# A transformer block on one Trainium2 core: part of the first shift and scale sums moved to TensorE, and the second half of them queued behind the first products

## The chip, the cores and the metric

The kernel runs on one core of a Trainium2 chip. The metric is device microseconds of one execution, the median of several runs. The core's engines appear under the names of the profile: PE is TensorE (PEld its weight loads), DVE is VectorE, ACT is ScalarE, POOL is GpSimd, SP is the engine that issues most DMAs.

## The reference

One layer of a block with 512 tokens of width 1024. A conditioning vector `c` gives shift, scale and gate vectors, the input is normalised and modulated by them, and one wide projection follows, which feeds two attention branches; a retrieval layer with 16384 single-neuron experts ends the block. Only the start matters here:

```
mod = silu(c) @ w_ada + b_ada                 # w_ada is 1024 x 6144
sh1, sc1, g1, sh2, sc2, g2 = split(mod, 6)
h = rms_norm(x, norm1_g) * (1 + sc1) + sh1    # 512 x 1024
proj = h @ w_in                               # 1024 contraction = 8 tiles of 128
```

So no element of `h` exists before its shift and scale are known, and each of these is a sum over 1024 rows of `w_ada`.

## The kernel before, in words

Loads. SP first asks for `x` (4 transfers) and then for the 2048 columns of `w_ada` that hold sh1 and sc1 (L166 to L174). These come in four chunks of 512 columns, in the order shift of the first half, scale of the first half, shift of the second half, scale of the second half (`i` = 0, 2, 1, 3). A chunk is four tiles `wa` of 512 KB; a tile holds two of the eight pieces `k` of the contraction. There are eight buffers for the sixteen `wa` tiles, so the tiles of the third and fourth chunk are asked for as those of the first two come free.

Sums. For a chunk (L284 to L299) POOL makes piece 0 times its `silu(c)` value (`accw`), DVE adds further pieces, one SCALAR_TENSOR_TENSOR of 128x512 each (L292), and TensorE sums over the 128 partitions: four matmuls of one column with `accw` as weights and a column of ones (L297). The pieces named in `PK` don't go through DVE: TensorE multiplies them directly, four matmuls of one column each, on the same line. In fp32 the trace shows eight instructions for four of these. A DVE reduce (L299) adds the parts up, and `ada_fin` (L216) adds the bias and, for a scale, forms (1 + scale) times the gain. Before, `PK = (1,)`: one piece in eight for every chunk.

Modulation. TensorE transposes the normalised `x` into eight contraction tiles `kt` (L267, four transposes each, two PSUM buffers), ACT copies each out to `xT` (L286). Once a shift and its scale are there, `mod_split` (L270) makes four of the tiles: DVE multiplies and adds (L274), ACT rounds the result to the high part `hh` (L91), DVE subtracts to get the low part `hl` (L92). Tiles 0 to 3 follow the first two chunks, tiles 4 to 7 the last two.

Products. `proj` (L378) takes the pieces of `w_in`, splits each into `whi` and `wlo` in the same way (L91, L92; low parts on POOL or DVE, `piece`, L370) and multiplies: for each of the eight contraction tiles, four row blocks by three matmuls of 512 columns (`mm3`, L84 to L88), so 12 products a tile and 96 in all for the first 512 columns (`v_chunk(1536, 512, ...)`, called at L674). All four PSUM tiles `pj` hold its sums until the eighth tile is done; then ACT copies them to `va` (L479) and the next chunk can begin.

Order. The program is written with the tile framework. Within an engine the instructions run in one fixed order, which the framework chooses when the program is built, from the order in the text and its own estimate of times; nothing is reordered on the chip but for weight loads pulled ahead. In the text the first projection comes far behind the sums, behind the rotary tables too.

Of the kernel before, what the change touches and what calls it, by code (L numbers as in the profile page):

```python
# [15 lines left out]
F32 = mybir.dt.float32  # L16
F32R = mybir.dt.float32r
# [43 lines left out]
def setup(tc, ctx, K):  # L61
# [22 lines left out]
    def mm3(ps, l, r, start, stop):  # L84
        (lh, ll), (rh, rl) = l, r
        nc.tensor.matmul(ps, lh, rh, start=start, stop=False)  # L86
        nc.tensor.matmul(ps, lh, rl, start=False, stop=False)  # L87
        nc.tensor.matmul(ps, ll, rh, start=False, stop=stop)  # L88

    def split(hi, lo, raw, eng=None):  # L90
        nc.scalar.activation(hi, raw, AF.Copy)  # L91
        (eng or nc.vector).tensor_tensor(lo, raw, hi.bitcast(F32), op=OP.subtract)  # L92

    def rsqrt(out, v, w):
        i = K.wk.tile([128, w], I32, name=f"rs_i{w}", bufs=2)
# [36 lines left out]
def front(K, A):  # L132
# [15 lines left out]
    def wraw():  # L148
        return wf.tile([128, 512], F32, name="raw", bufs=5)
# [120 lines left out]
    def mod_split(raws, col, dst, hook=None, kts=range(8)):  # L270
        for kt in kts:
            raw = raws(kt)
            t = f2()
            nc.vector.tensor_scalar(t, raw, col[:, 8 + kt:9 + kt], col[:, kt:kt + 1], op0=OP.mult, op1=OP.add)  # L274
            split(dst[0][:, kt, :], dst[1][:, kt, :], t)
            if hook is not None:
                hook(kt, t)

    norm_rows(xt, xt, "n1", st)
    PK = (1,)  # L280
    xT = st.tile([128, 8, 512], F32, name="xT")
    hT = K.big("h", ta)
    col1 = cst.tile([128, 16], F32, name="col1")
    for n, i in enumerate((0, 2, 1, 3)):  # L284
        for kt in range(2 * n, 2 * n + 4) if n % 2 == 0 else ():
            nc.scalar.activation(xT[:, kt, :], transpose_in(xt, kt, ptr()), AF.Copy)  # L286
        accw = st.tile([128, 512], F32, name="acc0", bufs=2)
        w = [wa[4 * n + k // 2][:, k % 2, :] for k in range(8)]
        nc.gpsimd.tensor_scalar(accw, w[0], sil[:, 0:1], 0.0, op0=OP.mult, op1=OP.add)
        for k in range(1, 8):  # L290
            if k not in PK:
                nc.vector.scalar_tensor_tensor(accw, w[k], sil[:, k:k + 1], accw, op0=OP.mult, op1=OP.add)  # L292
        p = pscore()
        sums = [(w[k], sil[:, k:k + 1]) for k in PK] + [(accw, ones[:, 0:1])]
# [71 lines left out]
    win = A['w_in'].rearrange("(k p) n -> p k n", p=128)  # L366
    nload = [0]
    ND1 = 20

    def piece(load, n, pool=None):  # L370
        raw = wraw()
        hi, lo = ((pool or wf).tile([128, 512], F32R, name=s, bufs=2 if pool else 4) for s in ("whi", "wlo"))
        load(raw)
        nload[0] += 1
        split(hi[:, :n], lo[:, :n], raw[:, :n], nc.gpsimd if nload[0] % 2 and not 8 <= nload[0] < ND1 else nc.vector)
        return hi[:, :n], lo[:, :n]

    def proj(lT, wv, c0, n, nk, done, jp=None):  # L378
        pss = [pmat()[:, :n] for _ in range(4)]
        for k in range(nk):  # L380
            if jp is None:
                w = piece(lambda raw: nc.sync.dma_start(raw[:, :n], wv[:, k, c0:c0 + n]), n)
            else:
                w = piece(lambda raw: nc.sync.dma_start(
                    raw[:, :n].rearrange("p (g i) -> p g i", g=3),
                    wv[:, k, c0:c0 + 768].rearrange("p (g j i) -> p g j i", g=3, j=2)[:, :, jp, :]), n)
            for a in range(4):
                at = slice(a * 128, a * 128 + 128)
                l = [t[k] if type(t) is list else t[:, k] for t in lT]
                mm3(pss[a], (l[0][:, at], l[1][:, at]), w, k == 0, k == nk - 1)  # L390
            yield 12 * 0.216 * n / 512
        for a in range(4):
            done(a, pss[a])

    att = Pool("att")
    oa = att.tile([128, 4, 256], F32, name="oa")
# [114 lines left out]
    for i in range(2):  # L511
# [4 lines left out]
            nc.gpsimd.memset(b[z, :], 0.0)  # L516
            q.append(b)
        qraw.append(q)
    va = dil.tile([128, 4, 768], F32, name="va")

    def k_raw(p):
        raw = dil.tile([128, 512], F32, name="kT", bufs=4)
# [33 lines left out]
    def dil_out(j, a, s, rz):  # L556
# [8 lines left out]
        for b in range(6):  # L565
            hd = (j, j, j, j, 4 + j, 8 + j)[b]
            kt = b if b < 4 else a
            nc.tensor.matmul(po[:, :64], eT[:, b * 128:b * 128 + 128], va[:, kt, hd * 64:hd * 64 + 64],
                             start=b == 0, stop=b == 5)
        nc.vector.tensor_scalar(oa[:, a, j * 64:j * 64 + 64], po[:, :64], rz, None, op0=OP.mult)  # L570

# [705 lines left out]
```

## Time and profile before

| | us |
|---|---|
| median of 3 runs | 2010.34 (2009.19 to 2011.33) |
| the profiled execution, its own time | 2011.68 |
| its span in the profile | 2009.8 |
| PE busy in the span | 1873.7 (93%) |
| DVE busy | 1593.2 (79%) |
| ACT busy | 842.7 (42%) |
| POOL busy | 698.0 (35%) |

The profile is of one execution. Its page gives the busy time of each engine, the span in 40 slices of 50.2 us with the busy share in tenths, and the granted TensorE clock in the same slices. A view of stretches gives the same for any part of the span; a view in order of time lists instructions with their start, their length (of a merged run of like instructions: from the first start to the last end), their line, and in brackets the time that the engine sat idle before them and what ended it.

### The profile page before, as it was taken

What the parts mean: (1) busy time and instruction counts of PE and PEld (TensorE: products, weight loads), DVE (VectorE), ACT (ScalarE), POOL (GpSimd) and SP (SyncE); (2) the same over time, 40 slices, a digit from 0 to 9 for tenths busy, and PEclk for the clock granted to TensorE, in tenths of its full rate; (3) what the DMA queues carried; (4) which work ended last, traced back from release to release, by engine and by line L of the source; (5) the groups of instructions that cost most, each with busy time, mean ns of one, the idle gap of its engine ahead of it and who ended that gap; (6) DMA issues with size and microseconds to landing.
All of it is one profiled execution on the core that took longest, in us unless ns stands there. A gap on an engine that the chain in (4) does not pass through costs nothing.

```text
span 2009.8 us, 28332 instructions
## 1 busy us (share of the span) xinstructions
PE 1873.7 (93%) x9858; PEld 1620.1 (81%) x9858; DVE 1593.2 (79%) x3276; ACT 842.7 (42%) x1330; POOL 698.0 (35%) x534
## 2 busy tenths in 40 slices
PE   6999998989899899999989999839999999999998
PEld 5987777778677788899989999828888888878886
DVE  7488585886775759999979989968778888888764
ACT  3444454645633333345545555513333333333342
POOL 2554332352235522012444147233234334323200
PEclk9999999999999999999999999969999999999999
DMA  7334242122256322468688979889999999999962
GB/s 262 86 120 121 63 145 60 35 87 84 59 152 215 128 72 81 147 226 276 229 295 316 322 274 322 299 287 371 360 320 354 342 354 330 355 361 325 345 225 93
DMA packets 206417, 447.30 MB, mean 223 GB/s; under 512 B 17297, under 2 KB 104642, under 8 KB 206146
## 3 DMA queue, kind: packets, MB, share of 16 engines
q1 hardware_dynamic: 168592, 309.14, 45.5%
q0 software_dynamic: 36864, 134.23, 18.8%
q10 hardware_dynamic: 818, 2.12, 0.3%
q8 instruction: 77, 1.26, 0.3%
q14 instruction: 66, 0.54, 0.1%
HBM read 397.20 MB, written 48.23 MB: 222 GB/s over the span
## 4 chain that ended last, share of the span: by engine, by line
PE 51%; DVE 16%; DMA 6%; issue 3%; ACT 2%; POOL 1%; SPq 0%; DVEq 0%; ACTq 0%; POOLq 0%
PE y L1220 26%; PE pj L86 7%; PE pj L87 7%; PE pj L88 7%; DMA raw<-uT 3%; DVE wlo L92 2%; DVE og L1130 2%; PE pg L1137 1%; DVE mr L933 1%; DMA raw<-w_ada 1%; DVE idx L935 1%; ACT whi L91 1%; DMA raw<-expert_v 1%; DVE oh L1125 1%; DVE idx L932 1%
## 5 line engine op out<-in xcount | busy, mean ns | idle before, releaser
L91 ACT ACTIVATE whi<-raw 128x1024 fp32r<-128x1024 f32 (+3 forms) x431 | 382.0, 893 | 382.6 <-PE pj L88 108.5
L92 DVE TENSOR_TENSOR wlo<-raw,whi 128x1024 fp32r<-128x1024 f32 (+3 forms) x339 | 376.9, 1114 | 98.1 <-ACT whi L91 96.7
L86 PE MATMUL pj<-h2h,whi 128*128 128x384 f32 x1008 | 345.8, 343 | 12.0 <-ACT am L879 10.9
L88 PE MATMUL pj<-h2h,wlo 128*128 128x384 f32 x1008 | 344.8, 342 | 5.0 <-DVE wlo L92 5.0
L87 PE MATMUL pj<-h2l,whi 128*128 128x384 f32 x1008 | 345.3, 343 | 0.0
L1058 POOL DMA_INDIRECT gat<-expert_v,eidx x128 | 211.9, 1656 | 316.9 <-DVE acc L1076 219.2
L1058 POOL DMA_INDIRECT gat<-expert_u,eidx x128 | 169.1, 1321 | 401.9 <-DVE gscr L1064 228.2
L1220 PE MATMUL y<-whi,ah 128*128 128x512 f32 x768 | 232.5, 397 | 33.3 <-ACT ah L91 28.4
L1220 PE MATMUL y<-wlo,ah 128*128 128x512 f32 x768 | 243.3, 397 | 0.7 <-DVE wlo L92 0.7
L92 POOL TENSOR_TENSOR wlo<-raw,whi 128x512 fp32r<-128x512 f32 (+2 forms) x92 | 146.5, 1598 | 278.7 <-ACT whi L91 256.0
L1220 PE MATMUL y<-whi,al 128*128 128x512 f32 x768 | 234.5, 395 | 0.0
L91 ACT ACTIVATE ah<-am 128x384 fp32r<-128x384 f32 x128 | 67.0, 524 | 333.5 <-PE y L1220 229.2
L86 PEld LDWEIGHTS pj<-h2h,whi 128*128 128x128 f32 x1008 | 192.2, 191 | 15.7 <-ACT am L879 12.9
L86 PE MATMUL pj<-whi,hh 128*128 128x512 f32 (+2 forms) x512 | 191.7, 387 | 9.8 <-DVE gA L651 4.4
L1220 PEld LDWEIGHTS y<-whi,ah 128*128 128x128 f32 x768 | 144.3, 189 | 67.7 <-ACT ah L91 28.6
L87 PE MATMUL pj<-wlo,hh 128*128 128x512 f32 (+2 forms) x512 | 196.2, 384 | 2.3 <-DVE wlo L92 2.3
L88 PEld LDWEIGHTS pj<-h2h,wlo 128*128 128x128 f32 x1008 | 191.9, 190 | 6.3 <-DVE wlo L92 6.3
L87 PEld LDWEIGHTS pj<-h2l,whi 128*128 128x128 f32 x1008 | 191.8, 190 | 1.1
L88 PE MATMUL pj<-whi,hl 128*128 128x512 f32 (+2 forms) x512 | 191.1, 380 | 0.0
L1220 PEld LDWEIGHTS y<-wlo,ah 128*128 128x128 f32 x768 | 144.7, 188 | 36.1 <-DVE wlo L92 1.2
L1220 PEld LDWEIGHTS y<-whi,al 128*128 128x128 f32 x768 | 144.2, 188 | 35.3
L1076 DVE SCALAR_TENSOR_TENSOR acc<-gat,wts,acc 128x1024 f32<-128x1024 f32 x127 | 162.4, 1279 | 9.6 <-DMA gat<-expert_v,eidx 9.2
(313 smaller groups left out, 3209.5 us busy)
## 6 DMA issues: line engine op xcount, KB each, us to landing
raw<-uT SPq DMA_DIRECT2D x128, 512.0 KB
raw<-expert_v SPq DMA_DIRECT2D x128, 512.0 KB
gd<-stage SPq DMA_DIRECT2D x48, 512.0 KB
gch<-gd SPq DMA_DIRECT2D x16, 1536.0 KB
raw<-w_in SPq DMA_DIRECT2D x88, 256.0 KB
am<-gls SPq DMA_DIRECT2D x96, 192.0 KB
gls<-am SPq DMA_DIRECT2D x94, 192.0 KB
raw<-w_ada SPq DMA_DIRECT2D x64, 256.0 KB
```

Of the source, the lines that this page charges most:

```text
L86: nc.tensor.matmul(ps, lh, rh, start=start, stop=False)
L87: nc.tensor.matmul(ps, lh, rl, start=False, stop=False)
L88: nc.tensor.matmul(ps, ll, rh, start=False, stop=stop)
L91: nc.scalar.activation(hi, raw, AF.Copy)
L92: (eng or nc.vector).tensor_tensor(lo, raw, hi.bitcast(F32), op=OP.subtract)
L932: nc.vector.max_index(out=i[:, 0:8], in_max=v[:, 0:8], in_values=s)
L933: nc.vector.match_replace(out=r, in_to_replace=v[:, 0:8], in_values=s, imm_value=-3.0e38)
L935: nc.vector.max_index(out=i[:, 8:16], in_max=v[:, 8:16], in_values=r)
L1058: nc.gpsimd.indirect_dma_start(out=t, out_offset=None, in_=src, in_offset=bass.IndirectOffsetOnAxis(ap=eidx[:, s:s + 1], axis=0))
L1076: nc.vector.scalar_tensor_tensor(acc, t, wts[:, s:s + 1], acc, op0=OP.mult, op1=OP.add)
L1130: nc.vector.tensor_tensor(o, oh[0].rearrange("p e t -> p t e"), gp[i][:, ts, None].to_broadcast([128, T, 128]), op=OP.mult)
L1220: nc.tensor.matmul(ys[b][n], l[:, bs], r[:, n * 512:n * 512 + 512], start=n_ == 0 and i == 0, stop=n_ == 127 and i == 2)
```

## The change

`PK` becomes a tuple for each chunk. For the first two chunks TensorE takes pieces 1, 3, 5 and 7 and DVE pieces 2, 4 and 6; for the last two it stays at piece 1. The first projection is made before the sums as a generator, and its steps are called in between: after the first two chunks three contraction tiles of it, then the third chunk, then the fourth contraction tile, then the fourth chunk. `issue_after(x)` gives each instruction that is traced inside an edge behind `x`, on `x`'s engine only: so what the third chunk does on TensorE (its sums, and the sixteen transposes of tiles 4 to 7) stands behind the last product of contraction tile 2, and what it does on DVE behind the low part of tile 1; the fourth chunk stands on TensorE behind the last product of tile 3, and on DVE behind the low part of tile 3 and behind the last addition of the third chunk. The other four steps of the projection are run where all eight were run before. Its functions `piece` and `proj` move up in the text unchanged, but that `proj` keeps the last product in `K.last`.

```diff
-        nc.tensor.matmul(ps, ll, rh, start=False, stop=stop)
+        return nc.tensor.matmul(ps, ll, rh, start=False, stop=stop)
...
-            split(dst[0][:, kt, :], dst[1][:, kt, :], t)
+            K.low.append(split(dst[0][:, kt, :], dst[1][:, kt, :], t))
...
-    PK = (1,)
+    PK = ((1, 3, 5, 7), (1, 3, 5, 7), (1,), (1,))
...
+    def first_products(n):
+        for _ in range(n):
+            next(first)
+
+    va = [None]
+    first = proj(hT, win, 1536, 512, 8, lambda a, ps: nc.scalar.activation(va[0][:, a, 0:512], ps, AF.Copy))
+
+    def ada1(n, i):
...
-            if k not in PK:
-                nc.vector.scalar_tensor_tensor(accw, w[k], sil[:, k:k + 1], accw, op0=OP.mult, op1=OP.add)
+            if k not in PK[n]:
+                K.sum = nc.vector.scalar_tensor_tensor(accw, w[k], sil[:, k:k + 1], accw, op0=OP.mult, op1=OP.add)
...
+    ada1(0, 0)
+    ada1(1, 2)
+    first_products(3)
+    with K.tc.issue_after(K.last.ins), K.tc.issue_after(K.low[1].ins):
+        ada1(2, 1)
+    first_products(1)
+    with K.tc.issue_after(K.last.ins), K.tc.issue_after(K.low[3].ins), K.tc.issue_after(K.sum.ins):
+        ada1(3, 3)
...
-    run(v_chunk(1536, 512, va[:, :, 0:512]))
-    run(v_chunk(2048, 256, va[:, :, 512:768]))
+    run(first)
+    run(v_chunk(2048, 256, va_[:, :, 512:768]))
```

## Rows read from the trace of the kernel before

**Rows 1.** The page, the span in 40 slices: busy tenths of PE and DVE, and the granted clock of TensorE in tenths of full speed.

```profile
PE   6999998989899899999989999839999999999998
...
DVE  7488585886775759999979989968778888888764
...
PEclk9999999999999999999999999969999999999999
```

**Rows 2.** The view of stretches, three of them one after the other: the start up to the first product, the products of contraction tiles 0 to 3, those of tiles 4 to 7 up to the next chunk's first. Columns: PE, PEld, DVE, ACT, POOL busy us (and instructions), granted clock, share of the DMA engines, GB/s.

```profile
10.44:31.24 20.80, 15.35 (x68) 14.09 (x69) 19.94 (x45) 9.18 (x16) 7.02 (x6) 1.00 1.05 388
31.24:49.18 17.94, 16.66 (x78) 13.57 (x78) 14.51 (x24) 4.61 (x9) 5.63 (x3) 1.00 0.34 116
49.18:64.22 15.04, 13.05 (x48) 10.09 (x48) 9.98 (x31) 6.88 (x14) 9.90 (x18) 0.89 0.22 54
```

**Rows 3.** The view in order of time, engine PE, from its first instruction to the first product: start, length, line, tiles, count, idle before.

```profile
10.47 1.84 PE L297 MATMUL ps<-sil,wa 128*128 128x1 f32 x8 [10.47 <-DMA wa<-w_ada]
12.24 0.37 PE L212 MATMUL pt<-ident,rows 64*128 64x64 f32 x1
15.79 1.87 PE L297 MATMUL ps<-sil,wa 128*128 128x1 f32 x8 [3.18 <-DMA wa<-w_ada]
17.52 1.84 PE L297 MATMUL ps<-ones,acc 128*128 128x1 f32 x8
19.23 1.95 PE L267 MATMUL pt<-ident,xt 128*128 128x128 f32 x8
21.43 2.12 PE L267 MATMUL pt<-ident,xt 128*128 128x128 f32 x8 [0.26 <-ACT xT L286]
25.53 1.86 PE L297 MATMUL ps<-ones,acc 128*128 128x1 f32 x8 [1.98 <-DVE acc L292]
27.26 1.09 PE L267 MATMUL pt<-ident,xt 128*128 128x128 f32 x4
28.15 1.71 PE L297 MATMUL ps<-sil,wa 128*128 128x1 f32 x8
29.71 1.95 PE L267 MATMUL pt<-ident,xt 128*128 128x128 f32 x8
31.31 0.78 PE L86 MATMUL pj<-whi,hh 128*128 128x512 f32 x1
```

**Rows 4.** The same view of PE later: what stands between the products of tiles 0 to 3, and the first product of tile 4.

```profile
37.86 0.60 PE L267 MATMUL pt<-ident,xt 128*128 128x128 f32 x4
38.29 0.95 PE L297 MATMUL ps<-sil,wa 128*128 128x1 f32 x8
39.10 0.94 PE L88 MATMUL pj<-whi,hl 128*128 128x512 f32 x3
...
46.15 0.95 PE L297 MATMUL ps<-ones,acc 128*128 128x1 f32 x8
46.96 0.48 PE L86 MATMUL pj<-whi,hh 128*128 128x512 f32 x1
...
49.18 0.63 PE L86 MATMUL pj<-whi,hh 128*128 128x512 f32 x1 [1.29 <-ACT hh L91]
```

**Rows 5.** The same view of DVE and ACT around the two modulations (additions of the second chunk, its reduce, the first modulation and its high parts; the additions of the third and fourth chunk; the reduce of the fourth).

```profile
21.26 4.22 DVE L292 SCALAR_TENSOR_TENSOR acc<-wa,sil,acc 128x512 f32<-128x512 f32 x3
...
27.43 0.17 DVE L299 TENSOR_REDUCE pr<-ps 128x4 f32<-128x8 f32 x1 [0.34 <-PE ps L297]
...
28.89 2.18 ACT L91 ACTIVATE hh<-f 128x512 fp32r<-128x512 f32 x4
...
33.59 7.80 DVE L292 SCALAR_TENSOR_TENSOR acc<-wa,sil,acc 128x512 f32<-128x512 f32 x9
...
47.13 0.17 DVE L299 TENSOR_REDUCE pr<-ps 128x4 f32<-128x8 f32 x1 [1.72 <-PE ps L297]
```

**Rows 6.** The view of one tile, `wa`: two of the groups that read it; count, shortest, median and longest ns, first and last start.

```profile
L297 PEld LDWEIGHTS ps<-sil,wa x32: 190/333/338, 10.4 to 39.0; 128*128 128x128 f32 x32
...
L292 DVE SCALAR_TENSOR_TENSOR acc<-wa,sil,acc x24: 739/752/1779, 12.2 to 41.9; 128x512 f32<-128x512 f32 x24
```

**Rows 7.** The view of stretches again, finer; columns as in rows 2.

```profile
31.24:36.00 4.76, 4.76 (x14) 3.74 (x14) 4.72 (x7) 0.91 (x2) 2.91 (x1) 1.00 0.97 352
36.00:47.90 11.90, 11.89 (x66) 9.83 (x64) 8.50 (x15) 2.49 (x4) 2.72 (x2) 1.00 0.12 35
47.90:49.18 1.28, 0.00 (x0) 0.00 (x1) 1.28 (x4) 1.20 (x3) 0.00 (x0) 1.00 0.00 0
49.18:53.60 4.42, 4.42 (x12) 3.49 (x13) 4.30 (x12) 1.51 (x3) 2.68 (x2) 0.61 0.24 64
53.60:62.20 8.60, 8.60 (x37) 6.60 (x36) 4.28 (x14) 4.33 (x7) 5.20 (x12) 1.00 0.27 59
```

**Rows 8.** The view in order of time where the first chunk of the projection hands over to the next: ACT's exponential for lambda, its copies to `va`, PE's next product.

```profile
63.18 0.20 ACT L359 ACTIVATE nlam<-nlam 128x2 f32<-128x2 f32 x1 [1.94 <-DVE nlam L358]
...
63.59 2.04 ACT L479 ACTIVATE va<-pj 128x512 f32<-128x512 f32 x4
...
64.22 0.38 PE L86 MATMUL pj<-whi,hh 128*128 128x256 f32 x1 [2.00 <-ACT va L479]
```

More of the change, by code (lines that the diff above doesn't have):

```diff
@@ L87, in mm3 @@
         nc.tensor.matmul(ps, lh, rl, start=False, stop=False)
-        nc.tensor.matmul(ps, ll, rh, start=False, stop=stop)
+        return nc.tensor.matmul(ps, ll, rh, start=False, stop=stop)
     def split(hi, lo, raw, eng=None):
         nc.scalar.activation(hi, raw, AF.Copy)
-        (eng or nc.vector).tensor_tensor(lo, raw, hi.bitcast(F32), op=OP.subtract)
+        return (eng or nc.vector).tensor_tensor(lo, raw, hi.bitcast(F32), op=OP.subtract)
+    K.low = []
     def rsqrt(out, v, w):
@@ L274, in mod_split, with piece, proj @@
             nc.vector.tensor_scalar(t, raw, col[:, 8 + kt:9 + kt], col[:, kt:kt + 1], op0=OP.mult, op1=OP.add)
-            split(dst[0][:, kt, :], dst[1][:, kt, :], t)
+            K.low.append(split(dst[0][:, kt, :], dst[1][:, kt, :], t))
             if hook is not None:
                 hook(kt, t)
+    win = A['w_in'].rearrange("(k p) n -> p k n", p=128)
+    nload = [0]
+    ND1 = 20
+    def piece(load, n, pool=None):
+        raw = wraw()
+        hi, lo = ((pool or wf).tile([128, 512], F32R, name=s, bufs=2 if pool else 4) for s in ("whi", "wlo"))
+        load(raw)
+        nload[0] += 1
+        split(hi[:, :n], lo[:, :n], raw[:, :n], nc.gpsimd if nload[0] % 2 and not 8 <= nload[0] < ND1 else nc.vector)
+        return hi[:, :n], lo[:, :n]
+    def proj(lT, wv, c0, n, nk, done, jp=None):
+        pss = [pmat()[:, :n] for _ in range(4)]
+        for k in range(nk):
+            if jp is None:
+                w = piece(lambda raw: nc.sync.dma_start(raw[:, :n], wv[:, k, c0:c0 + n]), n)
+            else:
+                w = piece(lambda raw: nc.sync.dma_start(
+                    raw[:, :n].rearrange("p (g i) -> p g i", g=3),
+                    wv[:, k, c0:c0 + 768].rearrange("p (g j i) -> p g j i", g=3, j=2)[:, :, jp, :]), n)
+            for a in range(4):
+                at = slice(a * 128, a * 128 + 128)
+                l = [t[k] if type(t) is list else t[:, k] for t in lT]
+                K.last = mm3(pss[a], (l[0][:, at], l[1][:, at]), w, k == 0, k == nk - 1)
+            yield 12 * 0.216 * n / 512
+        for a in range(4):
+            done(a, pss[a])
     norm_rows(xt, xt, "n1", st)
-    PK = (1,)
+    PK = ((1, 3, 5, 7), (1, 3, 5, 7), (1,), (1,))
     xT = st.tile([128, 8, 512], F32, name="xT")
@@ L283, in front @@
     col1 = cst.tile([128, 16], F32, name="col1")
-    for n, i in enumerate((0, 2, 1, 3)):
+    def first_products(n):
[4 more added lines that the diff above has]
+    def ada1(n, i):
         for kt in range(2 * n, 2 * n + 4) if n % 2 == 0 else ():
@@ L290, in front @@
         for k in range(1, 8):
-            if k not in PK:
-                nc.vector.scalar_tensor_tensor(accw, w[k], sil[:, k:k + 1], accw, op0=OP.mult, op1=OP.add)
+            if k not in PK[n]:
+                K.sum = nc.vector.scalar_tensor_tensor(accw, w[k], sil[:, k:k + 1], accw, op0=OP.mult, op1=OP.add)
         p = pscore()
-        sums = [(w[k], sil[:, k:k + 1]) for k in PK] + [(accw, ones[:, 0:1])]
+        sums = [(w[k], sil[:, k:k + 1]) for k in PK[n]] + [(accw, ones[:, 0:1])]
         for f, (l, r) in enumerate(sums):
@@ L363, in front @@
     st.close()
[L366 to L393, printed above, removed]
     att = Pool("att")
@@ L518, in front @@
         qraw.append(q)
-    va = dil.tile([128, 4, 768], F32, name="va")
+    va[0] = va_ = dil.tile([128, 4, 768], F32, name="va")
     def k_raw(p):
@@ L567, in dil_out @@
             kt = b if b < 4 else a
-            nc.tensor.matmul(po[:, :64], eT[:, b * 128:b * 128 + 128], va[:, kt, hd * 64:hd * 64 + 64],
+            nc.tensor.matmul(po[:, :64], eT[:, b * 128:b * 128 + 128], va_[:, kt, hd * 64:hd * 64 + 64],
                              start=b == 0, stop=b == 5)
```

## The prediction, written before the changed kernel was run

> **What bounds the kernel now.** Read the page's slices first: PE is at eight tenths or more in nearly all of them, DVE lower except in patches, and the first slice is the weakest of PE but for one in the middle [rows 1]. All that follows waits for data of the first products, and PE has few gaps in which a delay could vanish, so I let it be passed on whole. So the change is worth what it moves the first chunk of the projection, and next one reads the start alone, in stretches [rows 2].
>
> Up to the first product at 31.31, DVE is busy 19.94 of 20.80 us and PE 15.35; transfers run at 388 GB/s all the while, so they are also full. From there to the first product of tile 4, PE is busy 16.66 of 17.94 us: that stretch is PE's, though DVE's additions of the third and fourth chunk lie in it. The third stretch hangs on the second modulation.
>
> Now the order of time for PE [rows 3]. It waits 3.18 us for `w_ada` and 1.98 us for DVE's additions, and little else. Those two waits are what more work on PE could fill; but it must be seen how long that work takes. A direct piece, or an `accw` sum, is eight instructions; from one such group to the next thing on PE is 1.73, 1.71, 1.73 and 1.56 us. The same group between products takes 0.81 us (38.29 to 39.10, and 46.15 to 46.96) [rows 4]. The start is at the lower level: the granted clock shows 0.61 and the products 0.37 us apart in 49.18 to 53.60, against 0.23 us at clock 1.00 later, and the first products after 31.24 are 0.34 us apart too, although the clock row shows 1.00 there, having no earlier entry [rows 7]. From 25.53 to 31.31 PE goes from sums to transposes without a pause, and the groups stay at the long price [rows 3].
>
> **What the change does to the first half.** It takes three additions out of each of the first two chunks: six of DVE's 0.752 us [rows 6], 4.5 us, with three of them at the 1.4 us that the last ones took (4.22 for three) [rows 5]. It adds six direct pieces to PE: 6 x 1.72 = 10.3 us. Against that stand 5.2 us of waits, and the work that moves out from before the first product: one direct piece of the third chunk and twelve transposes, 27.26 to 31.31, 4.05 us [rows 3].
>
> Done as one sum from PE's first instruction, with PE never waiting: ten groups (two chunks of four direct and one `accw`) at 1.72 = 17.2 us, the small transpose of the bias rows 0.37, sixteen transposes 3.4 (eight in 1.60, four in 0.89) [rows 3]. 10.47 + 20.97 = 31.44. Can it go on without waiting? The first tile of the second chunk was there at 15.79 [rows 3]; three more of 0.524 MB at 388 GB/s [rows 2] are there by 19.8, and DVE with its last addition by 20.6. PE comes to these later in every order. So PE becomes the bound here and DVE's 4.5 us are off the path.
>
> Then the order counts. If the `accw` group of the second chunk is last, the reduce, the column, the modulation and the high part still follow: 2.08 us, as from the end of the group at 46.15 to the product at 49.18 [rows 4]. PE has nothing to fill it with, since the third chunk's work may not pass the products. First product at 33.52: 2.21 us later than before. If some ten transposes stand behind that group they fill it, and the product comes at 31.44. I take the first, since before too the sixteen transposes stood ahead of that group [rows 3]. Bounds: 1.56 a group and transposes behind, 29.6 (1.7 us earlier); 1.84 a group, 1.95 per eight transposes and the group last, 35.2 (3.9 later).
>
> A rule of the Trainium skill stands against this price: "TensorE: Matmul & The Clock Gate", section "LDWEIGHTS (loading the stationary operand)", gives columns / 1.2 ns for a weight load, 107 ns for 128 columns. By it eight loads would be 0.85 us, ten groups 8.5 us, and the first half would end far earlier. The loads here took 333 ns in the median, 190 at best [rows 6], so I go by the trace; what such a price would do is the fourth case below.
>
> **What it does to the second half.** Between first product and tile 4, PE had 48 products, four transposes, three groups, and 1.29 us of idle time [rows 4, 7]. Added are the twelve transposes that were done early (0.43 for four between products: 1.29 us) and the third chunk's direct group (0.81) [rows 4]. And the fourth chunk's two groups now stand behind every product of tile 3: before, three products filled part of the 2.08 us behind its last sum, now none does; 2.08 - 1.29 = 0.79 us. Sum 2.89 us.
>
> What covers the rest: DVE's twelve additions wait for the low part of tile 1, about 1.3 us after the first product. Twelve at 0.75 to 0.87 (nine in 7.80) [rows 5], two low parts and two of `w_in` at about 0.68, make them done 13.0 to 14.4 us after it; PE needs the last at 17.9 (48 products and what stands between them). Behind DVE's queued additions stand low parts of `w_in`, which the second half needs only after that. The transfers: the last `wa` buffers come free with the second chunk's pieces on PE, a few us later than before, but the channels were still full with requests and emptied only by about 36 [rows 7], and the data is needed past 45; SP's order of `w_in` against `w_ada` can shift without being felt. ACT's copies of the late transposes lie between products; if PE had to wait for them with two PSUM buffers, some 0.5 us, in the range.
>
> Tile 4 then starts 2.21 + 2.89 = 5.10 us later, and after it everything is as before: the drop of the clock to the lower level after the gap [rows 7] stays, and the rotary tables, lambda and the copies to `va` hang on the same fourth chunk [rows 8]. So 2011.68 + 5.1 = 2016.8 for a profiled execution; the runs' median was 1.3 below that one, so 2010.34 + 5.1 = 2015.4.
>
> **The other ways.** Second: the transposes fill the gap behind the second chunk's sum, and the delay is 0.13 + 2.89 = 3.0 us: 2013.4. A little can come back in the third stretch, where ACT's exponential at 63.18 holds up copies that could start when the products end at 62.2, 1.3 us [rows 8]: 2012.0 to 2013.4. For it: the framework will see those transposes as work for an idle PE. Against: they come first in the text.
>
> Third, worse: a stretch without products arises between tiles 2 and 3 (sixteen transposes and two groups, 3.3 us at the short price) and the granted clock falls there as it did at 49.18, after three products in 3 us [rows 4, 7]. A drop costs 4.42 us for what at 0.23 apart takes 2.8, and transposes at 0.89 instead of 0.43 for four: some 2.5 us, 2017.9. Additions at 1.41 us each [rows 5] would do much the same: DVE done at 20.9, 3 us late, 2018.4.
>
> Fourth, on the other side: PE's groups are cheap when they follow one another for 20 us, 0.81 each as between products. Then PE is done with the rest by the time that the last tile and DVE arrive (20.6), the last sum ends at 21.5, the first product comes at 23.6, 7.7 us earlier, and 2.89 later is given back: 2005.5; 2 us less again if the first products too start at the upper level. The point from which it decides: the first product must come before 31.31 - 2.89 = 28.42, so ten groups may take 12.1 us, 1.21 each. For it: the short price exists. Against: each group before the products that the trace shows took 1.56 or more, also in the stretch without a pause.
>
> That the edges do nothing can be set aside as a case of its own: without them PE's 10.3 us remain.
>
> **Chances.** First 0.48, second 0.24, third 0.14, fourth 0.14. The likeliest one's own range is 2012 to 2018.5. Of 0.2% (4.0 us, about what a measurement of this kernel can tell): slower, above 2014.4, are the third case and three quarters of the first, 0.50; within, the second and the rest, 0.37; faster, the fourth, 0.13. Leaving out half of the fourth and the far end of the third, and allowing a few us for another order of instructions behind the start, the range is 2006 to 2020.5.
>
> **What would show it.** In PE's order of time: ten groups of eight at about 1.7 us from 10.5 on with hardly a gap, the `accw` group of the second chunk ending near 31.4, the first product near 33.5, DVE idle before it. Then three tiles of products with transposes and groups behind them at 0.43 and 0.81, an idle gap of 2.1 us before tile 4 at about 54.3, and the clock falling there. The copies to `va` near 68.7, and from there on the old distances. Groups under 1.2 us, or a first product before 28.4, make the prediction wrong; so does a later stage that moves by more than 2 us against the start.

## The result, and the profile after

The changed kernel took 2021.73 us in the median of 7 runs (2019.23 to 2024.26), the kernel before 2011.18 in the runs beside it (7 runs): ratio 1.0051, 95% interval 1.0036 to 1.0066, so 10.2 us slower, 7.3 to 13.3. The forecast was 2015.4 in a range to 2020.5: the sign was right, the size was not, and the time fell out of the range by 1.2 us. The profiled execution took 2020.46 us by itself, 8.8 above that of before; it is the one read here.

First the order of time of PE from its first instruction to the first product of contraction tile 4 (answers to [rows 3, 4]; columns: start, length, line, tiles, count, idle before and what ended it).

```profile
11.27 2.27 PE L338 MATMUL ps<-sil,wa 128*128 128x1 f32 x10 [11.27 <-DMA wa<-w_ada]
...
13.76 4.85 PE L338 MATMUL ps<-sil,wa 128*128 128x1 f32 x22
18.47 1.09 PE L269 MATMUL pt<-ident,xt 128*128 128x128 f32 x4
19.35 1.71 PE L338 MATMUL ps<-sil,wa 128*128 128x1 f32 x8
...
23.37 3.55 PE L338 MATMUL ps<-sil,wa 128*128 128x1 f32 x16
...
29.99 1.85 PE L338 MATMUL ps<-ones,acc 128*128 128x1 f32 x8
34.12 0.80 PE L86 MATMUL pj<-whi,hh 128*128 128x512 f32 x1 [2.29 <-ACT hh L91]
...
44.58 1.04 PE L269 MATMUL pt<-ident,xt 128*128 128x128 f32 x8
45.45 0.95 PE L338 MATMUL ps<-sil,wa 128*128 128x1 f32 x8
...
51.72 1.03 PE L338 MATMUL ps<-ones,acc 128*128 128x1 f32 x8
54.64 0.50 PE L86 MATMUL pj<-whi,hh 128*128 128x512 f32 x1 [1.89 <-ACT hh L91]
```

Ten groups of eight and sixteen transposes follow one another without a gap, 1.57 to 1.72 us a group (22 instructions in 4.7 us, 16 in 3.4); the `accw` group of the second chunk is last, and behind it PE stands idle for 2.29 us. Between the products the same group costs 0.82. Ahead of tile 4 there is the second gap, 1.89 us.

DVE in the same stretch: its last addition of the second chunk, and the reduce that it then waits for.

```profile
20.70 0.75 DVE L333 SCALAR_TENSOR_TENSOR acc<-wa,sil,acc 128x512 f32<-128x512 f32 x1 [0.59 <-DMA wa<-w_ada]
...
31.87 0.18 DVE L340 TENSOR_REDUCE pr<-ps 128x4 f32<-128x20 f32 x1 [4.63 <-PE ps L338]
```

DVE is done with the sums at 21.4, where before it held PE up to 25.5; now it idles 4.63 us for PE. Then the hand-over to the next chunk of the projection, 5.09 us later than in [rows 8]:

```profile
69.31 0.38 PE L86 MATMUL pj<-whi,hh 128*128 128x256 f32 x1 [1.66 <-ACT va L323]
```

And the rest of the run, cut at six events that both traces have, from POOL's first work on the keys to PE's last matmul. Columns as in [rows 2]: length, busy us (and instructions) of PE, PEld, DVE, ACT, POOL, granted clock, DMA share, GB/s. Before:

```profile
100.80:542.00 441.20, 403.90 (x2151) 336.82 (x2150) 340.29 (x641) 234.46 (x493) 163.40 (x139) 0.98 0.29 84
542.00:715.10 173.10, 161.27 (x716) 129.41 (x715) 110.02 (x194) 55.10 (x91) 81.48 (x58) 0.96 0.49 161
715.10:914.80 199.70, 190.83 (x1004) 173.79 (x1003) 183.89 (x984) 71.74 (x99) 38.49 (x21) 0.98 0.44 141
914.80:1341.40 426.60, 383.57 (x2629) 361.74 (x2627) 382.92 (x650) 214.67 (x263) 163.88 (x79) 0.95 0.85 295
1341.40:2002.80 661.40, 652.53 (x2928) 544.05 (x2928) 511.51 (x668) 226.68 (x310) 209.66 (x171) 0.99 0.89 316
```

After:

```profile
105.90:551.20 445.30, 405.52 (x2151) 338.27 (x2150) 340.49 (x641) 234.41 (x492) 163.00 (x139) 0.97 0.28 84
551.20:726.00 174.80, 159.76 (x716) 127.83 (x716) 109.03 (x195) 55.11 (x91) 81.92 (x58) 0.97 0.49 159
726.00:925.00 199.00, 190.21 (x1011) 173.69 (x1010) 183.82 (x985) 72.12 (x100) 38.07 (x21) 0.99 0.45 141
925.00:1349.20 424.20, 382.69 (x2622) 361.36 (x2620) 382.32 (x649) 214.77 (x263) 171.69 (x79) 0.95 0.85 295
1349.20:2011.50 662.30, 652.60 (x2928) 542.81 (x2928) 513.58 (x668) 227.26 (x310) 234.50 (x171) 0.99 0.89 317
```

The changed kernel is 5.1 us late at 100 us, 9.2 at 542, 10.9 at 715, 10.2 at 915, 7.8 at 1341 and 8.7 at the end. So about half of the loss is the start, as forecast, and the rest seems to come in the first two rows. In the first PE is busy 1.62 us longer with the same instructions and idles 2.5 us more (445.30 - 405.52 against 441.20 - 403.90). The order of the instructions on every engine is the same in both kernels from about 72 to 1349 us, so this is no new work. Behind 1349 us it is not the same: the framework chose another order there for the changed kernel, and compared place by place 356 of PE's instructions and 350 of DVE's are others. What the loss behind the start is, was the main question to the experiments.

### The profile page after: what moved, and what is told of

Same layout as the page of the kernel before. It is cut to its first block, busy times and chain, and to the rows that moved or that the text cites. A ratio compares the mean times of both kernels' runs of the same rounds, so it can differ in the third digit from the quotient of the medians.

```text
span 2018.2 us, 28427 instructions
## 1 busy us (share of the span) xinstructions
PE 1879.6 (93%) x9906; PEld 1626.8 (81%) x9906; DVE 1591.7 (79%) x3270; ACT 843.7 (42%) x1330; POOL 727.5 (36%) x534
## 3 DMA queue, kind: packets, MB, share of 16 engines
q1 hardware_dynamic: 168592, 309.14, 45.5%
## 4 chain that ended last, share of the span: by engine, by line
PE 53%; DVE 15%; DMA 6%; issue 3%; ACT 2%; POOL 1%; SPq 0%; DVEq 0%; ACTq 0%; POOLq 0%
PE y L1240 24%; PE pj L86 8%; PE pj L87 8%; PE pj L88 8%; DVE wlo L92 2%; PE pg L1157 2%; DMA raw<-uT 2%; DMA raw<-expert_v 1%; DMA raw<-w_ada 1%; DVE mr L953 1%; ACT whi L91 1%; DVE idx L955 1%; DVE idx L952 1%; DVE acc L1096 1%; DVE og L1150 1%
## 5 line engine op out<-in xcount | busy, mean ns | idle before, releaser
L1078 POOL DMA_INDIRECT gat<-expert_v,eidx x128 | 234.6, 1833 | 290.0 <-DVE acc L1096 188.3
L1078 POOL DMA_INDIRECT gat<-expert_u,eidx x128 | 177.7, 1389 | 392.1 <-DVE gscr L1084 208.1
L1096 DVE SCALAR_TENSOR_TENSOR acc<-gat,wts,acc 128x1024 f32<-128x1024 f32 x127 | 162.4, 1279 | 11.4 <-DMA gat<-expert_v,eidx 10.9
```

Of the source, the lines that this page charges most:

```text
L1078: nc.gpsimd.indirect_dma_start(out=t, out_offset=None, in_=src, in_offset=bass.IndirectOffsetOnAxis(ap=eidx[:, s:s + 1], axis=0))
L1096: nc.vector.scalar_tensor_tensor(acc, t, wts[:, s:s + 1], acc, op0=OP.mult, op1=OP.add)
```

## The experiments

| kernel | first product | hand-over | ratio to the kernel before, 95% interval |
|---|---|---|---|
| before, first trace | 31.31 | 64.22 | |
| before again (e1) | 28.88 | 61.26 | 1.000, 0.9985 to 1.0016 |
| the change | 34.12 | 69.31 | 1.0051, 1.0036 to 1.0066 |
| the change again (e2) | 33.62 | 69.32 | 1.0051, 1.0032 to 1.007 |
| tuple alone (e3) | 39.26 | 65.51 | 1.0026, 1.001 to 1.0041 |
| order alone (e4) | 28.98 | 63.47 | 1.0012, 0.9999 to 1.0025 |
| change, no edges (e5) | 37.89 | 69.30 | 1.0036, 1.002 to 1.0053 |
| change, DVE adds again (e6) | 33.65 | 69.92 | 1.0057, 1.004 to 1.0074 |
| change, seven groups (e7) | 28.23 | 62.96 | 0.9999, 0.9977 to 1.002 |
| change, PE warmed (e8) | 32.55 | 67.15 | 1.0054, 1.0033 to 1.0075 |
| change, sums as rows (e9) | 29.57 | 64.76 | 1.0016, 0.9998 to 1.0034 |
| rows, PE warmed (e10) | 29.77 | 65.64 | 1.0055, 1.0035 to 1.0075 |
| before, start late (e11, e13, e16) | 35.77, 35.75, 35.68 | 67.13, 66.96, 66.95 | 1.000, 1.0039, 1.0015 (each about 0.0018 either way) |
| before, start later (e12) | 39.28 | 71.46 | 1.0082, 1.0059 to 1.0106 |
| before, start latest (e15) | 44.11 | 76.89 | 1.0099, 1.0075 to 1.0124 |
| rows for one chunk, no gap (e14) | 30.53 | 64.84 | 1.0017, 0.9998 to 1.0036 |

First product and hand-over (first product of the next chunk) are us in one profiled execution each.

### Both kernels again

> The kernel before, unchanged, run again for a second trace and as a measure of the noise. All theories: ratio 1.000, interval about plus or minus 0.0015. In its trace the first product at 31.3 us and the first product of contraction tile 4 at 49.2 us, each within 0.5 us. If the delay that the changed kernel showed beyond the 5.1 us of the start is only where the drops of the granted clock fall, this trace differs from the first trace of before by 2 us or more in the stretch from 100 to 1300 us.

> The changed kernel, unchanged, run again. Theory (a delay of 5.1 us made before tile 4, the rest an accident of one execution): first product near 34, tile 4 near 54.6, and the time between 5 and 7 us above before, ratio 1.0025 to 1.0035. Rival (something behind the start is slower in every execution): ratio 1.005 again, and the same stretches between 100 and 1300 us or behind 1350 us late again by the same amounts.

The times came out again (2011.06 and 2019.74 in the median). For the changed kernel that is the ratio of the rival, 1.0051, and not the 1.0025 to 1.0035 of the theory; stretch by stretch it is neither. The first two stretches are long again (444.2 and 175.9 us), but the fourth is 8.4 us longer than in the first trace of the same kernel (432.7 against 424.3). The expectation for the kernel before missed at the start, which is not one thing. PE in its second trace:

```profile
19.50 1.95 PE L267 MATMUL pt<-ident,xt 128*128 128x128 f32 x8
21.70 2.12 PE L267 MATMUL pt<-ident,xt 128*128 128x128 f32 x8 [0.26 <-ACT xT L286]
24.68 1.05 PE L297 MATMUL ps<-ones,acc 128*128 128x1 f32 x8 [0.85 <-DVE acc L292]
25.59 0.64 PE L267 MATMUL pt<-ident,xt 128*128 128x128 f32 x4
26.06 0.95 PE L297 MATMUL ps<-sil,wa 128*128 128x1 f32 x8
26.87 1.72 PE L267 MATMUL pt<-ident,xt 128*128 128x128 f32 x8
```

Behind the sixteen transposes a group takes 0.91 us (24.68 to 25.59) where [rows 3] has 1.73: the granted clock was at its upper level from 23.7 to 27.1 us. The first product came 2.43 us earlier, 0.85 of it because DVE's last addition was done earlier (the group starts at 24.68 in place of 25.53), the other 1.58 behind it. The order-only run did the same in part (its group of eight at 25.65 took 1.33). In the changed kernel the transposes stand in fours between the groups, and in none of its two traces does the clock rise ahead of the products.

### The tuple without the order, and the order without the tuple

```diff
e3, before with
-    PK = (1,)
+    PK = ((1, 3, 5, 7), (1, 3, 5, 7), (1,), (1,))
e4, after with
-    PK = ((1, 3, 5, 7), (1, 3, 5, 7), (1,), (1,))
+    PK = ((1,), (1,), (1,), (1,))
```

> Only the tuple PK as in the change; program order as before, no edges, first projection where it was. Theory (PE's one-column groups at 1.7 us bound the first half): the planned order puts all sums and transposes ahead of the first product, thirteen groups and 32 transposes, so the first product comes near 41 us and tile 4 near 54 to 55 us, about 5 us later than before: 2015 to 2018 us. Rival (the edges and the late transposes cost the time, the groups fill idle time): 2011 us or less, tile 4 at 49 us or earlier.

> The changed kernel with PK = (1,) for all four chunks: only the new order with its edges. Theory: with four groups fewer on each side the first product is set by DVE's additions as before and comes at about 29.5 to 30.3 us, since a group and twelve transposes have moved behind it; then 20.5 us to tile 4, near 50.5 us: 1 to 2 us above before, 2012 to 2013 us, ratio 1.0005 to 1.001. Rival (edges are the cost): tile 4 at 54 us and 2020 us.

Both times came out as the theories had them (2016.5 and 2012.8). Against the first trace of before the tuple alone costs 1.3 us at the hand-over, not 5: all transposes and all sums but the fourth chunk's last go ahead of the first product (39.26), and then there is neither a gap ahead of tile 4 nor a fall of the clock there. The order alone gives 0.75 us back. Only together are they 5.1. Against the mean of the two traces of before (62.74) the three figures are 2.8, 0.7 and 6.6 us later; either way the two together cost more than their sum. The reading that fits: the order takes one group and the late transposes out of a start that PE binds, and pays for it with the gap ahead of tile 4.

### The change without its edges

```diff
-    with K.tc.issue_after(K.last.ins), K.tc.issue_after(K.low[1].ins):
-        ada1(2, 1)
+    ada1(2, 1)
...
-    with K.tc.issue_after(K.last.ins), K.tc.issue_after(K.low[3].ins), K.tc.issue_after(K.sum.ins):
-        ada1(3, 3)
+    ada1(3, 3)
```

> The change without its edges: the tuple of pieces stays, the first projection is made early, but nothing holds the third and fourth chunk's sums behind products. Theory (what the edges do is keep six groups and the late transposes out of the start, and what they cost is the gap before tile 4): the sums come first again, first product near 39 us, hand-over of the first chunk near 65.5, no drop of the granted clock before tile 4, time as with the tuple alone, 2016 to 2018. Rival (the loss behind the start comes from the moved projection itself, not from the edges): first product near 39, but 2020 or more.

Missed. The sums did come first but for the fourth chunk's last and part of the third's (first product 37.89), but the hand-over is at 69.30, as with the edges, because the gap stayed. PE ahead of tile 4:

```profile
51.65 0.39 PE L88 MATMUL pj<-whi,hl 128*128 128x512 f32 x1
51.88 0.95 PE L338 MATMUL ps<-ones,acc 128*128 128x1 f32 x8
55.26 0.50 PE L86 MATMUL pj<-whi,hh 128*128 128x512 f32 x1 [2.42 <-ACT hh L91]
```

The fourth chunk's last sum still stands behind all of tile 3's products. In the tuple-only run, also without edges, there was no such gap: so it is the place of the projection's first tiles in the text, ahead of the third and fourth chunk, that makes it, and the edges change nothing that is left at the hand-over.

### What binds the start: DVE, the number of groups, or their price

```diff
e6
+    dump = st.tile([128, 512], F32, name="dump")
...
+            elif n < 2 and k > 1:
+                nc.vector.scalar_tensor_tensor(dump, w[k], sil[:, k:k + 1], w[k], op0=OP.mult, op1=OP.add)
e7
-    PK = ((1, 3, 5, 7), (1, 3, 5, 7), (1,), (1,))
+    PK = ((1, 3, 5), (1, 3), (1,), (1,))
e8
+    wide = st.tile([128, 512], F32, name="wide")
+    nc.gpsimd.memset(wide, 1.0)
+    pw_ = ptr()
+    for _ in range(WARM):
+        nc.tensor.matmul(pw_, ones, wide, start=True, stop=True)
```

> The changed kernel in which DVE does again, into a scratch tile, the six additions that went to TensorE (their result is not used): the work that the change took from DVE is given back to it. Theory (PE's one-column groups are the bound of the start, DVE's relief is worth nothing): first product within 0.7 us of 34.1, hand-over 68.7 to 70, time 2020 to 2023. Rival (DVE is still the bound and its relief paid for part of PE's work): first product at 36 or later, time 2 us or more above the changed kernel.

DVE, with its six additions back, still waits for PE, and the first product is no later (33.65):

```profile
24.17 0.74 DVE L337 SCALAR_TENSOR_TENSOR dump<-wa,sil 128x512 f32<-128x512 f32 x1
...
31.70 0.18 DVE L344 TENSOR_REDUCE pr<-ps 128x4 f32<-128x20 f32 x1 [5.59 <-PE ps L342]
```

So what the change took from DVE was worth nothing in the changed order. The time is 1.2 us above the changed kernel's by the ratios (1.0057 against 1.0051), well within both intervals.

> The changed order with fewer direct pieces: 1, 3, 5 in the first chunk, 1, 3 in the second, one in the others: seven groups ahead of the first product in place of ten. Theory (1.72 us a group and PE never waiting): 3 x 1.72 = 5.2 us earlier than the changed kernel, first product near 29, tile 4 near 49.3, hand-over near 64, time 2011 to 2014. Rival (DVE, with three additions more, becomes the bound): first product 30.5 to 32, time 2014 to 2017.

First product 28.23, 5.9 us before the changed kernel's, for three groups fewer (5.2 at 1.72); tile 4 at 48.92, and the time is that of the kernel before. Both runs say that PE's groups are the bound.

> The changed kernel with six float32 products of 512 columns on constant tiles put on the idle PE ahead of the first sum (their result is not used; some 10 us of PE's time before the first tile lands). Theory (a group's 1.72 us is the lower level of the clock, 0.81 us the upper one, and PE reaches the upper one after a stretch of wide products): the first groups take 0.8 to 0.95 us, the last sum of the second chunk is bound by transfers and DVE's additions (done at 21.4), first product 24 to 29 if the clock stays up, 30 to 32 if it falls again within some us; time 2011 to 2018. Rival (the price of a group is its own, one column after a load of weights, whatever the clock): groups at 1.7 us, first product 34 to 35, time 2021 to 2023.

```profile
1.46 7.77 PE L194 MATMUL pt<-wide,ones 128*128 128x512 f32 x12 [1.46 <-POOL wide L191]
10.45 1.02 PE L344 MATMUL ps<-sil,wa 128*128 128x1 f32 x8 [1.23 <-DMA wa<-w_ada]
...
13.85 3.58 PE L344 MATMUL ps<-sil,wa 128*128 128x1 f32 x16 [0.45 <-DMA wa<-w_ada]
17.28 1.09 PE L275 MATMUL pt<-ident,xt 128*128 128x128 f32 x4
```

The price of a group is the clock: 1.02 us for the first one behind the wide products, and 1.7 again (16 in 3.43) once the granted clock fell at 13.0, while PE did one-column products and waited for tiles. The start moved as in the expected case in which the clock falls again (32.55), but the time did not follow, 2022.4 where at most 2018 was expected. Its interval overlaps the changed kernel's.

### The sums as rows

```diff
+        if n < 2:
+            line = pmat()
+            sums = [(sil[:, k:k + 1], w[k]) for k in PK[n]] + [(ones[:, 0:1], accw)]
+            for f, (l, r) in enumerate(sums):
+                nc.tensor.matmul(line[0:1, :], l, r, start=f == 0, stop=f == len(sums) - 1)
+            flat = st.tile([1, 512], F32, name="flat", bufs=2)
+            nc.scalar.activation(flat, line[0:1, :], AF.Copy)
+            pr = pscore()
+            for j in range(4):
+                nc.tensor.matmul(pr[:, j:j + 1], flat[0:1, j * 128:j * 128 + 128], ones[0:1, 0:1], start=True, stop=True)
```

> The changed kernel with the sums of the first two chunks in another form: the column of scales is the stationary operand and the piece moves, 512 columns wide, so that all five pieces add up in one row of PSUM; the row is copied by ACT and turned into four columns by four one-row products, and DVE's reduce goes. Theory (the groups were dear because the clock stayed at its lower level under one-column products; wide ones cost the same at that level, 2 x 0.85 us a piece, but bring the clock up): the clock rises before the first product, pieces cost 0.86 us from there, first product 26 to 30, hand-over 61.5 to 65.5, time 2008 to 2016. Rival (wide pieces don't raise it before the products either): ten pieces at 1.7 us and 1.5 us for the turn into columns, first product 34 to 36, time 2021 to 2025.

```profile
10.71 3.57 PE L338 MATMUL pj<-wa,sil 128*1 128x512 f32 x4 [10.71 <-DMA wa<-w_ada]
...
17.71 1.02 PE L338 MATMUL pj<-wa,sil 128*1 128x512 f32 x2
...
24.86 1.02 PE L338 MATMUL pj<-acc,ones 128*1 128x512 f32 x2
26.83 1.05 PE L343 MATMUL ps<-ones,flat 1*128 1x1 f32 x8 [0.94 <-ACT flat L340]
29.57 0.60 PE L86 MATMUL pj<-whi,hh 128*128 128x512 f32 x1 [1.70 <-ACT hh L91]
```

A piece is now two instructions and costs about what it did as a group of eight at the same level: 1.75 us at first (four instructions in 3.5), 0.86 later. But while columns 512 wide ran the clock rose, at 16.2, and stayed up until 29.8. The same ten sums now cost 4.5 us less at the first product and at the hand-over (64.76), and the time can no longer be told from that of the kernel before (1.0016, 0.9998 to 1.0034).

> The rows of the run before, and six float32 products of 512 columns on constant tiles on the idle PE ahead of the first piece, as in the warmed run. Theory: the clock is up when the first piece lands and holds under wide pieces, so transfers and DVE's additions (done near 21.5) set the start: first product 24.5 to 27, tile 4 45 to 48, hand-over 60 to 63, time 2006 to 2013, at or under the kernel before. Rival (PE's waits for tiles let the clock fall as at 13.0 in the warmed run): first product 29 to 33, time 2014 to 2020.

Missed: the hand-over came at 65.64, no earlier than without the warming. PE waited for the first tiles (2.43 us ahead of 10.81), and the clock fell at 11.4. The time is far above that of the rows alone, and its trace has lost it late: 382.6 us from 546.60 to 929.20, where the kernel before has 372.8 (173.10 + 199.70). Why this kernel should lose there is not known. The two warmed kernels are both slower than their hand-overs say: against 62.74 they hand over 4.4 and 2.9 us later (e8, e10), by the ratios they end some 11 us later. That is not explained.

### Does a later start reach the end?

The kernel before, its start delayed by loads alone (e11, e13, e16; e12 and e15 the same with the loads two and four times):

```diff
+    xT = st.tile([128, 8, 512], F32, name="xT")
+    for a in range(4):
+        nc.sync.dma_start(xT[:, 2 * a:2 * a + 2, :].rearrange("p k n -> p (k n)"), xv[:, a, :])
     for a in range(4):
         nc.sync.dma_start(xt[:, a, :], xv[:, a, :])
```

> The kernel before with its start delayed by transfers alone: x is loaded once more, 2.1 MB into a tile that is overwritten later, ahead of the loads of x and w_ada, some 5.4 us at 388 GB/s. Nothing of the change is in it. Question: the changed kernel is 5.1 us later at the hand-over and some 10 at the end. Theory (what comes on top is partly a drop of the clock at 117 that belongs to the moved order and partly landings that differ from run to run): no drop near 115, the delay of the hand-over (4.5 to 6) is found again at 900 within 3 us, time 2015 to 2019. Rival (any delay of the start grows on the way, since something behind it is tied to a time and not to the start): 2.5 to 5 us more at 900 than at 100, time 2019 to 2023.

> The single delay once more, for a second trace and a narrower interval. Theory (passed on): 2015 to 2019 in the median. Rival (taken up behind): 2010 to 2014, and the second trace again loses its lateness behind 1300.

> The single delay a third time. Passed on (the first job was the outlier): ratio to the kernel before 1.002 to 1.005. Taken up: 0.999 to 1.001.

> The kernel before with its start delayed by 4.2 MB of loads in place of 2.1 (x twice more, one after the other). Theory (a later start is passed on, and the single delay's 0 at the end was spread): hand-over 10 to 14 us late, time 2020 to 2028. Rival (something behind the start takes lateness up, so that the start is not on the path of the end at all): hand-over as late, time 2009 to 2016.

> The kernel before with its start delayed by 8.4 MB of loads (x four times more). The single and the double delay came 2.8 and 7.2 us late at the hand-over, so some 16 to 18 here. Passed on whole: 16 to 18 us at the end, 2027 to 2029. Whole and a constant 4 us: 2031 to 2033. Growing by half on the way: 24 to 27 us, 2035 to 2038. Taken up behind: under 2022.

The hand-over of the kernel before is at 62.74 in the mean of its two traces. The single delay is 4.3 us later there, and 0, 7.8 and 3.0 us slower at the end (mean 3.6): one kernel, compared three times, so this is how far apart single results with such intervals lie. The double one is 8.7 later and 16.5 slower (11.9 to 21.3), the latest 14.2 later and 19.9 slower (15.1 to 25.0). So the long delays are not taken up behind; they reach the end with 7.8 and 5.7 us on top, though nothing of the change is in them. Both hand over less late than was expected (10 to 14, and 16 to 18). The latest came out where "whole and a constant 4 us" had been put (2031.04). Of the three single delays only the second came out as a delay passed on was expected to.

The single delay is not a pure delay. Behind 1349 us the framework chose another order for it than for the kernel before, and its last stretch took 658.5, 658.5 and 658.8 us in its three traces, where the two of before have 661.4 and 662.5. The second of them:

```profile
1344.70:2003.30 658.60, 651.18 (x2928) 542.62 (x2928) 513.75 (x668) 227.26 (x310) 229.56 (x171) 1.00 0.89 318
```

So some 3 us of the single delay went there, with another order; that the order is the cause is not shown. The latest delay is the cleanest test: it keeps the order of before but for 17 places of PE.

The expectation that no clock drop near 115 would show without the moved order also fell: two of the three single delays have one (at 116.2 and 115.9).

### The version to which this pointed

Rows in the first chunk only, and the fourth chunk's sums ahead of tile 3's products:

```diff
-        if n < 2:
+        if n < 1:
...
-    first_products(1)
     with K.tc.issue_after(K.last.ins), K.tc.issue_after(K.low[3].ins), K.tc.issue_after(K.sum.ins):
         ada1(3, 3)
+    first_products(1)
```

> Rows for the first chunk's sums only (they bring the clock up while the first tiles land), one-column groups for the second, and the fourth chunk's sums ahead of contraction tile 3's products in place of behind them, so that these cover the reduce, the modulation and the high part. Expected from the rows run and the kernel before: second chunk's last group at 24.5, first product 26.5 to 28.5, no gap ahead of tile 4, which starts at 42.5 to 46, hand-over 57.5 to 61.5, 3 to 6 us earlier than in the kernel before; time 2005 to 2009 if the start is passed on, 2010 to 2014 if not.

```profile
44.63 1.14 PE L269 MATMUL pt<-ident,xt 128*128 128x128 f32 x8
45.56 1.86 PE L349 MATMUL ps<-ones,acc 128*128 128x1 f32 x8
47.28 0.77 PE L86 MATMUL pj<-whi,hh 128*128 128x512 f32 x1
```

Missed. The gap ahead of tile 4 is gone, but 24 one-column products and 16 transposes now stand in one run (from 41.16) between the products, eight more behind them, and at 45.5 the clock fell for twice as long as it does at the gap; the hand-over is at 64.84. It also fell at 21.6 under the second chunk's one-column groups, so the first product came 2 us later than expected. No version tried here beats the kernel before.

## Why the prediction was wrong, step by step

**The bound and the first half.** Right. PE binds the start, DVE's relief is worth nothing (e6), a group costs 1.57 to 1.72. First product 34.12 against 33.52: the first tile landed 0.8 later (11.27 against 10.47), and what followed took 0.2 less than the sum.

**The second half.** Right: from first product to tile 4 20.52 us against 17.87, so 2.65 for the 2.89 forecast, with the gap (1.89 us for 2.08) and the fall of the clock where they were put. Tile 4 at 54.64 (54.3 forecast), the copies to `va` at 68.68 (68.7). Both traces of the change give a hand-over within 0.01 us of each other, 5.09 and 5.10 above [rows 8]; the sum for it was 5.10. That it fits to 0.01 us is in part luck: the parts are 2.81, 2.65 and -0.37 (tile 4 to hand-over) in the first trace and 2.31, 2.92 and -0.13 in the second, where 2.21, 2.89 and nothing were forecast.

**The price and the rule.** The Trainium skill, "TensorE: Matmul & The Clock Gate", section "LDWEIGHTS (loading the stationary operand)", would make it an estimated 107 ns a load. By their length the loads here took more. Shortest, median and longest ns:

```profile
L338 PEld LDWEIGHTS ps<-sil,wa x80: 188/333/338, 11.2 to 51.6; 128*128 128x128 f32 x80
```

The loads up to 29.7 us took 333 ns, at the lower level of the clock, and those from 45.3 on 188 to 192, at the upper one; no float32 load of 128 columns came near 107. The float16 loads of the same trace did, with 117 ns in the mean:

```profile
L1157 PEld LDWEIGHTS <-oh 128*128 128x128 f16 x768 | 50.5, 117 | 33.6 <-issue 19.8 <-DVE og L1150 11.0 <-DVE oh L1145 1.6
```

But the loads overlap. From start to start a group of eight took 0.82 us behind 45 us, 0.10 a load, and 1.71 in the run at 13.76, 0.21 a load. So by starts the price after the Trainium skill, an estimated 0.85 us for eight, is near that of the upper level, and twice as much was paid at the lower one; the prediction compared it with the length alone. It read the price rightly as the clock's. What it lacked is that the same sums in another form were followed by the upper level (e9).

**"The groups stay at the long price."** This step failed for the kernel before. I took one execution's start for the kernel's. In its second trace the run of sixteen transposes was followed by the upper level, and its first product came at 28.88. The mean hand-over of the two is 62.74, and against that the change is 6.6 later, not 5.1: 1.5 us of the error, as far as two traces tell. Of all seven traces with the start of before (the delayed ones are five) two show the upper level ahead of the products, the second of before and e12.

**"All passed on whole", and "after it everything is as before".** This is the step that failed for the rest: the prediction put nothing for all that comes behind the hand-over, and 10.2 less 6.6, so 3.6 us of the loss, came there as the medians have it. The long delays show that a later start is not taken up; that all stays as before they do not show, since they too end later than their hand-over says. What the 3.6 us are is in part open. In the two profiled executions 4.1 us came between 100 and 551 us, and 1.6 of these are one more fall of the clock. Here the granted clock (column before the last two) around the same idle of PE, 0.62 and 1.57 us in which it waits for POOL's keys, in the trace before,

```profile
110.00:112.00 2.00, 0.49 (x4) 0.49 (x5) 2.00 (x4) 1.31 (x4) 1.79 (x2) 1.00 0.00 0
112.00:114.00 2.00, 2.00 (x13) 1.96 (x12) 2.00 (x5) 0.54 (x2) 2.00 (x2) 1.00 0.33 98
```

and after:

```profile
116.00:118.00 2.00, 1.40 (x6) 1.40 (x7) 2.00 (x4) 0.67 (x2) 2.00 (x3) 0.74 0.01 4
118.00:120.00 2.00, 2.00 (x8) 2.00 (x8) 1.86 (x7) 0.38 (x1) 1.22 (x1) 0.50 0.33 98
```

The same instructions, the same idle, but eight of them in 2 us in place of thirteen, and what follows is 1.53 us later. Ten of the eighteen traces have this fall (the change, e2, e4 to e8, e11, e12, e16), eight have not (the two of before, e3, e9, e10, e13, e14, e15). Neither the order nor the delay decides it by itself, since e11 and e13 are one kernel. The other 2.5 us are idle time of PE. About half of it hangs on one landing. First DVE waits for it, where before there was no wait at all, and 7.99 us later, the same distance as before, PE waits for ACT, again where before there was no wait:

```profile
156.96 0.75 DVE L207 SCALAR_TENSOR_TENSOR acc<-raw,sil,acc 128x512 f32<-128x512 f32 x1 [1.26 <-DMA raw<-w_ada]
...
164.95 0.66 PE L581 MATMUL pt<-ident,s 128*128 128x128 f32 x4 [1.29 <-ACT s L571]
```

SyncE's queue issued its load at 152.42, 4.5 us ahead; in the trace before, 3.2 us were enough for the same addition not to wait.

Is this the change's doing? Over all eighteen traces the length of each of the five stretches is, by least squares, a constant plus 0.8 to 1.2 times PE's idle time plus 0.3 to 0.4 us for each us at the lower clock; what is left over has a standard deviation of 0.3 to 0.6 us. The seven traces in which POOL starts on the keys by 102.2 us have 444.0 us in the first of them in the mean (441.2 to 446.3), and the profiled execution of before is the shortest of all eighteen. The eleven that start later have 444.8 (442.8 to 448.2). In the second stretch it is 172.2 against 174.1, in the other three the means lie within 0.3. So in the means the later kernels take some 2 us more, most of it between 542 and 715, and of the 4.1 us that the two traces seemed to show the larger part is a lucky execution on the side of before. That lateness itself makes these 2 us is not shown: the three single delays are late as well and have 171.5, 171.2 and 173.7 us in that stretch. Worked out anew: 6.6 us at the hand-over and 2 behind it are 8.6, inside the interval of the time (7.3 to 13.3).

One rival was not tested: the other order of the last stretch, for which the prediction had allowed a few us in its range but nothing in its sum. The three traces that have the changed kernel's order there (the change, e2, e6) took 662.3, 665.0 and 663.3 us, before 661.4 and 662.5, so 1.6 us more in the mean. But e4 and e5, which also share one order there, differ by 4.7 us, so this too is not shown. The cause of the 3.6 us behind the hand-over stays open.

**The rivals.** The fourth (cheap groups) lacked its condition: the clock. At the start it rises under one-column products in none of the traces. The third put a further fall of the clock between tiles 2 and 3; the further fall came at 117, for 1.5 us. The run times did end nearest to the third's, 2018, by another way. The second, transposes behind the last sum, did not happen; they stand ahead of it.

## What to carry to other kernels

Work that is moved to an idle TensorE is priced at the clock that it will find there: sums of one column cost twice as much at the start as between products, and the clock did not rise while they ran, but it rose while the same sums ran with the piece as the 512-wide moving operand. The long delays at the start reached the end whole and with 6 to 8 us on top, and between two executions of one kernel a stage behind the start differed by up to 3 us, the one from 915 to 1341 us by up to 8: so a base for a sum of 5 us needs more than one trace of the kernel before. And a change at the start can move the order that the framework chooses far behind it; it is worth comparing the order of the whole run.

## What was not expected of the hardware

Whether the same idle of 2.2 us of PE is followed by the lower clock differs between executions of one kernel (e11 and e16 against e13), for 1.5 us each time. Sixteen transposes in a run of 4 us were followed by the upper level in one trace of before and not in the other. And one-column products, which count as busy in the profile, were followed by a fall in e8 (13.0) and e14 (21.6 and 45.5).
